# Twelve seven-product blocks instead of ten in the first feed-forward of an encoder layer, with a gate weight split earlier and the modulation work re-timed

## The chip, the cores and the metric

The kernel runs on one core of one Trainium2 chip. The metric is the device time in microseconds of one execution; lower is better.

## The reference

One layer of a streaming encoder on 544 tokens (512 of a prompt, 32 of a sample), width 1024. Shift, scale and gate vectors for three sublayers come from a conditioning vector per sequence:

```python
mod = silu(c) @ w_cond + b_cond                  # 9 pieces of 1024
sh1, sc1, gt1, sh2, sc2, gt2, sh3, sc3, gt3 = split(mod, 9)
x = LN(ALPHA*x + 0.5*(1+gt1) * swiglu(x*(1+sc1)+sh1, f1_gate, f1_up, f1_down))   # d_ff = 2816
x = LN(ALPHA*x +     (1+gt2) * mixer(x*(1+sc2)+sh2, w_in) @ w_out)
x = LN(ALPHA*x + 0.5*(1+gt3) * swiglu(x*(1+sc3)+sh3, f2_gate, f2_up, f2_down))

def swiglu(h, w_gate, w_up, w_down):
    return (silu(h @ w_gate) * (h @ w_up)) @ w_down
```

The mixer has four retention heads and eight heads of attention over keys that an indexer selects (at most 128 or 136 per query), all fed by one input projection `w_in` of 33 column blocks of 128. Everything is float32.

## The kernel before

**Layout and precision.** Activations lie transposed: 128 features on the partitions, 544 tokens along the free axis, in two halves of 272. A float32 operand is kept as two parts, `hi` and `lo`, and each product of a 128x128 weight block with 272 tokens is three matmuls (hi·hi, hi·lo, lo·hi). One pass of eight weight blocks over one half is so 24 matmuls.

**Weights.** `ensure`, `next_w` and `split_w` stream 128-column weight blocks: SyncE (SP) loads the raw block, ScalarE (ACT) casts it to `hi`, then either ScalarE writes the negated `hi` into `lo` and a DMA issued by GpSimd (POOL) adds the raw weight from memory onto it, or VectorE (DVE) subtracts. `next_w(n)` sees to it that n blocks beyond the one asked for have been given out for splitting; the default is `AHEAD = 3`. Split blocks lie in a pool `wh` of five buffers; most other large tiles (activations, residual, hidden blocks, modulation weights) are units of a pool `up` of 35.

**Seven products.** A feed-forward has 22 blocks f of 128 hidden features. An ordinary block (`ffn_mm` four times: gate and up, two halves each) is 96 matmuls. For the blocks in `SEVEN[0]` (first feed-forward, f = 6 to 15) and `SEVEN[1]` (second, f = 4 to 21), `feed` takes gate and up weight, split in two along the input features, with the two token halves as a 2x2 problem and does it by seven products of 12 matmuls (Strassen's scheme in Winograd's form), 84 in all. For this, activation sums (`sums`, once) and weight sums (`weight_sums`, four VectorE additions in place on the raw weights, then `split_sums`, two splits) are made. In `seven(f)` the products come in this order, each 12 matmuls: C (gate weight `Wg`), onto A (`Wg2`), B (`Wu2`), onto A (`Wu2`), A of the next block (`begin`, its `Wg`), onto A (`Wg2`), onto B (`Wu`, written `wh_u`). Short copies of A by ScalarE (`snapshot`, L713) and additions by VectorE (L763, L780, L794) take results out between them; a bank is written again only after these have read it. Inside `feed` the order of the ScalarE and VectorE instructions is pinned by hand. `make_gate(f)` is the cast (L683), the negation (L678) and the accumulating DMA (L679, tile `wh_g`) of a block's gate weight; in steady state it runs for block f + 2 at the start of block f. Ahead of the first seven-product block (`first7`), `make_gate(first7)` runs in block first7 - 2, and `make_gate(first7 + 1)`, `weight_sums(first7)` and `split_sums` in block first7 - 1. The results of these blocks stay unsplit in `flat` tiles, two to a unit; `split_flat` splits one per tick after the last seven-product block.

**Order.** The program is written out in one order; `tick()` is called after every pass of products, and jobs (generators given to `spawn`) resume at ticks and yield the number of ticks to their next step. A seven-product block has four ticks, as an ordinary block has. All SP loads, and all TensorE instructions, stay in program order; other instructions are placed by a scheduler with the program's order as priority.

**Modulation.** `cond` computes pieces 2 to 6 of `mod` on VectorE: per piece eight steps (one for each 128 rows of `w_cond`), each two multiply-adds of 128x1024 (L589; the first step of a piece L587), then `cond_done`: one tick apart four transposes with a sum each (L552, L553), and four ticks later a small matmul (`cc`). A list of gaps sets the ticks between steps. Piece 7 is made by `cond_ahead` during the input projection, piece 8 later. `consts` turns finished pieces into coefficients.

**After the feed-forward** come its down-projection (`proj_residual`, tile `dn`, residual tiles `xa` loaded by `scaled_residual`), the layer norm into `h2`, the input projection (`project`, tile `in`) interleaved with retention, indexer, selection and attention (`lg` are its logits), the output projection and the second feed-forward.

Of the kernel before, what the change touches and what calls it, by code (L numbers as in the profile page):

```python
# [18 lines left out]
ND = D // P  # L19
# [5 lines left out]
NF = FF // P  # L25
# [6 lines left out]
SEGS = ((((0, HT), 0),), (((HT, TP), 0), ((TP, T), 1)))  # L32
DOWN_G = ((0, 8), (8, 15), (15, 22))
AHEAD = 3
SEVEN = ((6, 15), (4, NF - 1))
WHOLE = (2, 8)


# [1 line left out]
def encoder_layer_kernel(ctx, tc, xT, cT, wc1, w_e, w_cond, b_condT, lnp, w_gu1, w_dn1, w_in, w_out, w_gu2, w_dn2,  # L40
# [32 lines left out]
    def load(*a):  # L73
        ordered("load", nc.sync.dma_start(*a))
# [12 lines left out]
    def resume(job, base):  # L87
        n = next(job, None)
        if n is not None:
            jobs.append((base + n, job))  # L90

    def spawn(job):
        resume(job, now[0] + 1)
# [14 lines left out]
    lp = const.tile([P, 6, ND], F32, name="lp")  # L108
# [8 lines left out]
    def mod(r, m):  # L117
        return modT[:, r, 8 * m:8 * m + 8]
# [42 lines left out]
    def ensure(n):  # L161
        while len(split) < n and stream and stream[0]:
            if not fetched:
                fetch_ahead()
            src, cnt, kw = stream.pop(0)
            split.append(split_w(fetched.pop(0), cnt, "w", src=src, **kw))

    def next_w(ahead=AHEAD):
        ensure(1 + ahead)
        return split.pop(0)  # L170
# [209 lines left out]
    def small(name):  # L380
        return const.tile([P, ND], F32, name=name)

    def mod_consts(n, msh, msc, lg, lb):
        G, B = [], []
        for r in range(2):
            g, bb = small(f"G{n}{r}"), small(f"B{n}{r}")
            nc.vector.tensor_scalar(g, mod(r, msc), 1.0, None, op0=ALU.add)
            nc.vector.tensor_mul(bb, g, lb)
            nc.vector.tensor_add(bb, bb, mod(r, msh))
            nc.vector.tensor_mul(g, g, lg)  # L390
            G.append(g)
            B.append(bb)
        return G, B

    def gate_coef(n, m, c):
        out = []
        for r in range(2):
            g = small(f"C{n}{r}")
            nc.vector.tensor_scalar(g, mod(r, m), c, c, op0=ALU.mult, op1=ALU.add)
            out.append(g)  # L400
        return out
# [12 lines left out]
    def queue_ffn(w_gu, w_dn, first):  # L414
        for f in range(2, NF):
            seven = SEVEN[0 if first else 1]
            if not seven[0] <= f <= seven[1]:
# [148 lines left out]
    def cond(parts, gaps):  # L566
        todo = [(m, d) for m in parts for d in range(ND)]
        ws, accs = [], {}

        def fetch():  # L570
            if len(ws) < len(todo):
                m, d = todo[len(ws)]
                ws.append(up.tile([P, 1024], F32, name=f"wc{m}_{d}", tag="u"))
                load(ws[-1], w_cond[d * P:(d + 1) * P, 1024 * m:1024 * m + 1024])

        fetch()
        yield 1
        fetch()
        yield 2
        for n, (m, d) in enumerate(todo):  # L580
            if d == 0:
                accs[m] = [up.tile([P, 1024], F32, name=f"ca{m}_{r}", tag="u") for r in range(2)]
            fetch()
            for r, acc in enumerate(accs[m]):
                c = cz[:, d, r:r + 1]
                if d == 0:
                    got = nc.vector.tensor_scalar(acc, ws[n], c, None, op0=ALU.mult)  # L587
                else:
                    got = nc.vector.scalar_tensor_tensor(acc, ws[n], c, acc, op0=ALU.mult, op1=ALU.add)  # L589
                tc.add_manual_dep(got.ins, last["pe"], NOSYNC, reason="pace")  # L590
            if d == ND - 1:
                spawn(cond_done(m, accs[m]))
            yield gaps[n % len(gaps)]

    def cond_ahead(m):
        acc = [up.tile([P, 1024], F32, name=f"ca{m}_{r}", tag="u") for r in range(2)]

        def part(d):
            return w_cond[d * P:(d + 1) * P, 1024 * m:1024 * m + 1024]

        def add(d, w):
            for r in range(2):
                c = cz[:, d, r:r + 1]
                if d == 0:
                    n = nc.vector.tensor_scalar(acc[r], w, c, None, op0=ALU.mult)
                else:
                    n = nc.vector.scalar_tensor_tensor(acc[r], w, c, acc[r], op0=ALU.mult, op1=ALU.add)
                tc.add_manual_dep(n.ins, last["pe"], NOSYNC, reason="pace")

        ws = [up.tile([P, 1024], F32, name=f"wc{m}_{d}", tag="u") for d in range(4)]  # L610
        for d in range(4):
            nc.gpsimd.dma_start(ws[d], part(d))
        yield 6
        for d in range(4):
            add(d, ws[d])
            yield 1
        yield 14
        for d in range(4, ND):
            ws.append(up.tile([P, 1024], F32, name=f"wc{m}_{d}", tag="u"))
            load(ws[d], part(d))  # L620
        for d in range(4, ND):
            add(d, ws[d])
            yield 5 if d < ND - 1 else 5
        spawn(cond_done(m, acc))

    def later(n, job):
        yield n
        yield from job

    def known(*ms):  # L630
        assert all(("mod", m) in flags for m in ms), ms
# [33 lines left out]
    def feed(h, hid, sums, flat, begun, gu, blocks, whole, lead=None):  # L665
# [4 lines left out]
        def load_gate(f):  # L670
            raw_g[f] = fetch_w(gu[f, 0], ND, "g")
# [9 lines left out]
        def make_gate(f):  # L681
            Wg[f] = wh.tile([P, 2, ND, P], FR, name="wh_g", tag="wh")
            pin(nc.scalar.copy(Wg[f][:, 0], raw_g[f]))  # L683
            negated(Wg[f][:, 0], Wg[f][:, 1], gu[f, 0])
# [31 lines left out]
        first7, last7 = blocks  # L716
# [92 lines left out]
        for f in range(2, first7):  # L809
            place(f)  # L810
            if f == first7 - 2:
                load_gate(first7)
                load_up(first7)
            if f == first7 - 1:
                load_gate(first7 + 1)
                load_up(first7 + 1)
                load_gate(first7 + 2)
            st = [None, None], {}
            for which in range(2):
                for i in range(2):  # L820
                    ffn_mm(st, h, which, i)
                    if f == first7 - 2 and which == 0:
                        if i == 0:
                            make_gate(first7)
                        else:
                            make_up(first7, 0)
                            make_up(first7, 1)
                    if f == first7 - 1:
                        if which == 0 and i == 1:
                            weight_sums(first7)  # L830
                        if which == 1 and i == 0:
                            split_sums(first7, Wg2, raw_g)
                            split_sums(first7, Wu2, raw_u)
                            make_gate(first7 + 1)
            for i in range(2):
                ffn_act(st, hid[f] if f < whole else None, i, flat.get(f))
        assert stream.pop(0) is None
# [12 lines left out]
        for i in range(2):  # L850
            ffn_act(sts[f], hid[f], i)
    flat, following = {}, ([None, None], {})
    spawn(later(4, cond((2, 3, 4, 5, 6), [3] * 4 + [4] * 10 + [2] * 12 + [2, 3] * 7)))
    feed(h, hid, sums, flat, None, w_gu1, SEVEN[0], WHOLE[0], lambda: ffn_mm(following, h, 0, 0))
    hid.extend([None] * len(flat))

# [7 lines left out]
    spawn(split_flat())  # L864
    for f in range(SEVEN[0][1] + 1, NF):
        hid.append(unit("hid", FR))
# [9 lines left out]
    G2, B2, C2, G3, B3 = [], [], [], [], []  # L876

    def consts(ready, *made):
        while not flags.issuperset(("mod", m) for m in ready):
            yield 1  # L880
        for dst, src in made:
            for got, new in zip(dst, src()):
                got.extend(new)

    spawn(consts((3, 4), ((G2, B2), lambda: mod_consts(2, 3, 4, lp[:, 0, :], lp[:, 1, :]))))
    spawn(consts((5, 6, 7), ((G3, B3), lambda: mod_consts(3, 6, 7, lp[:, 2, :], lp[:, 3, :])),
                 ((C2,), lambda: [gate_coef(2, 5, 1.0)])))

    h, rs, fin = ln_to_h(xr, G2, B2, "h2_", 4, 1)
    proj_residual(hid, xr, C1, DN, fin, ahead={(6, 15): 7, (7, 0): 6, (7, 8): 5, (7, 15): 4})  # L890
# [2 lines left out]

    xd = nc.dram_tensor("x_spill", [4, P, 2 * T], F32, kind="Internal").ap()

    def project(evac):
        hl = next_w()
        for i, (a, b) in enumerate(HALVES):
            ps = bank("a", "in")[:, :HT]
            for k in range(ND):  # L900
                mm3(ps, hl, k, h[k], a, b, k == 0, k == ND - 1)
            evac(ps, a, b)
            tick()
# [562 lines left out]
        tick()  # L1466


    known(5, 6, 7)
    h, rs, fin = ln_to_h(xr, G3, B3, "h3_", 3, 4)  # L1470
    proj_residual(mixed, xr, C2, OUT, fin, [("sample", 1)], ahead={(d, 0): min(5, 11 - d) for d in range(ND)})

# [38 lines left out]
    spawn(later(9, cond((8,), [4])))  # L1511
    feed(h, hid, sums, flat, begun, w_gu2, SEVEN[1], WHOLE[1])
    for f in range(WHOLE[1], NF):
# [155 lines left out]
```

## Time and profile before

| | us |
|---|---|
| median of 3 runs | 1152.5 |
| lowest and highest run | 1150.21, 1157.97 |
| the profiled execution, its own time | 1150.75 |
| span of that execution in the trace | 1149.0 |

The mean granted TensorE clock over the span was 0.993 of full speed. Times of instructions are counted from the start of the span; about 1.75 us of the execution lie around it. PE is TensorE's matmuls, PEld its weight loads, which run beside them. In the rows below, "xN" counts instructions that are merged into one row, and a bracket gives the idle time of the engine just before the row and what ended it. A PE row's length contains the pipeline's tail, so rows of PE overlap a little; the chain's rows do not.

### The profile page before, as it was taken

How to read it: one execution, taken by the hardware profiler on the slowest of the kernel's cores; microseconds unless marked ns; L12 is line 12 of the kernel's file. 1: busy time of each engine (PE TensorE's matmuls, PEld its weight loads, DVE VectorE, ACT ScalarE, POOL GpSimd, SP SyncE). 2: the span in 40 equal slices, each digit the busy share in tenths (PEclk: the TensorE clock that was granted, in tenths of full speed). 3: DMA queues.
4: the chain of work that ended last, by engine and by line, in shares of the span. 5: the costliest groups of instructions: out<-in, count | busy, mean ns of one | idle time of the engine just before them, and what ended most of it. 6: DMA issues, size and time to landing. Idle time of an engine off the chain costs nothing.

```text
span 1149.0 us, 22815 instructions
## 1 busy us (share of the span) xinstructions
PE 1116.0 (97%) x9083; PEld 1082.9 (94%) x9083; DVE 835.3 (73%) x1758; ACT 635.8 (55%) x1102; POOL 195.2 (17%) x219
## 2 busy tenths in 40 slices
PE   8998999999999999999989999999999999999995
PEld 7998999999999999989979989999999999999995
DVE  5576898686679686788999777789699976810416
ACT  3644666651434345765655758645666666753523
POOL 0110111111110301523211100100111111051110
PEclk9998999999999999999999999999999999999998
DMA  9897778985997547765954767871888687478742
GB/s 359 268 269 200 190 214 208 294 244 160 315 277 173 138 177 149 193 173 138 265 130 104 178 226 203 213 219 19 211 234 221 153 191 184 131 218 183 172 82 79
DMA packets 71452, 222.75 MB, mean 194 GB/s; under 512 B 8656, under 2 KB 12880, under 8 KB 71344
## 3 DMA queue, kind: packets, MB, share of 16 engines
q1 hardware_dynamic: 49456, 151.02, 37.6%
q0 software_dynamic: 21744, 70.13, 34.0%
q8 instruction: 71, 1.16, 0.4%
q14 instruction: 37, 0.30, 0.1%
q10 hardware_dynamic: 144, 0.14, 0.0%
HBM read 209.66 MB, written 9.58 MB: 191 GB/s over the span
## 4 chain that ended last, share of the span: by engine, by line
PE 74%; DMA 8%; DVE 8%; issue 6%; ACT 2%; SPq 0%; POOL 0%; DVEq 0%; POOLq 0%; ACTq 0%
PE dn L77 24%; PE in L77 12%; PE pA L77 11%; PE gu L77 11%; PE pB L77 5%; DMA we_raw<-in_w_e 3%; PE pC L77 3%; PE gu_e L77 2%; DMA wh_g<-in_w_gu 2%; DMA aqk<-rp 1%; DMA wc<-in_w_cond 1%; DMA wh_w<-in_w_dn 1%; DVE wh_s L702 1%; PE isc L77 1%; PE po L77 1%
## 5 line engine op out<-in xcount | busy, mean ns | idle before, releaser
L77 PE MATMUL dn<-hid,wh_w 128*128 128x272 f32 x2112 | 267.2, 288 | 0.7 <-DMA wh_w<-in_w_dn 0.5
L77 PEld LDWEIGHTS dn<-hid,wh_w 128*128 128x128 f32 x2112 | 265.4, 188 | 1.3 <-DMA wh_w<-in_w_dn 0.7
L77 PE MATMUL in<-h,wh_w 128*128 128x272 f32 x1392 | 187.0, 291 | 1.4 <-DMA wh_w<-in_w_in 1.4
L77 PEld LDWEIGHTS in<-h,wh_w 128*128 128x128 f32 x1392 | 176.6, 188 | 6.9 <-issue 3.5
L131 ACT CAST wh_w<-wr_w 128x1024 fp32r<-128x1024 f32 (+1 forms) x106 | 107.1, 1015 | 114.3 <-PE dn L77 75.9
L77 PE MATMUL gu<-h,wh_w 128*128 128x272 f32 x1152 | 145.2, 288 | 0.0
L77 PEld LDWEIGHTS gu<-h,wh_w 128*128 128x128 f32 x1152 | 144.6, 188 | 0.0
L589 DVE SCALAR_TENSOR_TENSOR ca<-wc,cz,ca 128x1024 f32<-128x1024 f32 x84 | 106.5, 1290 | 0.0
L77 PE MATMUL pA<-hs,wh_s 128*128 128x272 f32 x672 | 94.0, 289 | 1.5 <-ACT s L713 1.4
L77 PEld LDWEIGHTS pA<-hs,wh_s 128*128 128x128 f32 x672 | 87.4, 188 | 2.4 <-ACT s L713 2.4
L138 ACT ACTIVATE wh_w<-wh_w 128x1024 fp32r<-128x1024 f32 (+1 forms) x86 | 87.9, 1027 | 1.7
L286 DVE SCALAR_TENSOR_TENSOR xs<-dn,C,xs 128x272 f32<-128x272 f32 (+2 forms) x24 | 9.0, 404 | 81.6 <-PE dn L77 81.6
L679 POOL DMA_DIRECT2D wh_g<-in_w_gu x28 | 24.4, 871 | 232.0 <-ACT wh_g L678 129.4
L713 ACT COPY s<-pA 128x272 f32<-128x272 f32 x84 | 32.1, 382 | 55.5 <-PE pA L77 54.8
L139 POOL DMA_DIRECT2D wh_w<-in_w_dn x32 | 28.2, 880 | 165.8 <-ACT wh_w L138 120.1
L77 PE MATMUL pA<-h,wh_g 128*128 128x272 f32 x336 | 48.4, 293 | 5.3 <-DMA wh_g<-in_w_gu 5.3
L77 PEld LDWEIGHTS pA<-h,wh_g 128*128 128x128 f32 x336 | 45.0, 192 | 5.7 <-DMA wh_g<-in_w_gu 5.7
L139 POOL DMA_DIRECT2D wh_w<-in_w_in x29 | 25.3, 873 | 136.1 <-ACT wh_w L138 78.1
L77 PE MATMUL pA<-h,wh_s 128*128 128x272 f32 x336 | 47.4, 291 | 0.0
L702 DVE TENSOR_TENSOR wh_s<-wr_g,wh_s 128x1024 fp32r<-128x1024 f32 x28 | 34.3, 1224 | 17.3 <-ACT wh_s L701 17.3
L77 PE MATMUL pC<-h,wh_g 128*128 128x272 f32 x336 | 46.5, 287 | 0.0
L77 PE MATMUL pB<-hs,wh_u 128*128 128x272 f32 x336 | 46.4, 287 | 0.0
(329 smaller groups left out, 2022.2 us busy)
## 6 DMA issues: line engine op xcount, KB each, us to landing
wc<-in_w_cond SPq DMA_DIRECT2D x52, 512.0 KB, 6.1
wr_w<-in_w_in SPq DMA_DIRECT2D x33, 512.0 KB, 5.3
wh_w<-in_w_in POOLq DMA_DIRECT2D x29, 512.0 KB, 6.6
wr_w<-in_w_gu SPq DMA_DIRECT2D x28, 512.0 KB, 6.9
wr_g<-in_w_gu SPq DMA_DIRECT2D x28, 512.0 KB, 3.5
wr_u<-in_w_gu SPq DMA_DIRECT2D x28, 512.0 KB, 4.4
wh_g<-in_w_gu POOLq DMA_DIRECT2D x28, 512.0 KB, 6.5
wr_w<-in_w_dn SPq DMA_DIRECT2D x32, 448.0 KB, 3.9
```

What stands on the lines that cost most here:

```text
L77: ordered("pe", nc.tensor.matmul(*a, **kw))
L131: c = nc.scalar.copy(hi[:, :n, :], raw[:, :n, :])
L138: nc.scalar.mul(lo[:, :n, :], hi[:, :n, :].bitcast(F32), -1.0)
L139: nc.gpsimd.dma_start(lo[:, :n, :], src, accum_op=ALU.add)
L286: nc.vector.scalar_tensor_tensor(x[:, sa:sb], ps[:, sa - a:sb - a], coef[r][:, d:d + 1], x[:, sa:sb], op0=ALU.mult, op1=ALU.add)
L589: got = nc.vector.scalar_tensor_tensor(acc, ws[n], c, acc, op0=ALU.mult, op1=ALU.add)
L679: nc.gpsimd.dma_start(lo, src, accum_op=ALU.add)
L702: pin(nc.vector.tensor_tensor(W[f][:, 1], raw[f], W[f][:, 0].bitcast(F32), op=ALU.subtract))
L713: pin(nc.scalar.copy(s, ps))
```

## The change

- `SEVEN[0]` becomes (6, 17): twelve blocks of the first feed-forward by seven products instead of ten; four ordinary blocks follow instead of six.
- `make_gate(first7 + 1)` moves two passes earlier, ahead of `weight_sums(first7)` and `split_sums`. This is inside `feed` and so in both feed-forwards.
- The gaps of `cond` change: six ticks instead of four after piece 2's last step, four and three after steps 14 and 15, and two throughout after that.
- The last yield of `cond_ahead` is 20 instead of 5: piece 7's `cond_done` starts 15 ticks later.
- The coefficients that need piece 5 alone are made apart from those that need 6 and 7, and an assertion at build time that all three are known is dropped.
- The first three calls of `project` ask for four weights ahead instead of three.

```diff
-SEVEN = ((6, 15), (4, NF - 1))
+SEVEN = ((6, 17), (4, NF - 1))
...
         for d in range(4, ND):
             add(d, ws[d])
-            yield 5 if d < ND - 1 else 5
+            yield 5 if d < ND - 1 else 20
         spawn(cond_done(m, acc))
...
                     if f == first7 - 1:
+                        if which == 0 and i == 0:
+                            make_gate(first7 + 1)
                         if which == 0 and i == 1:
                             weight_sums(first7)
                         if which == 1 and i == 0:
                             split_sums(first7, Wg2, raw_g)
                             split_sums(first7, Wu2, raw_u)
-                            make_gate(first7 + 1)
...
-    spawn(later(4, cond((2, 3, 4, 5, 6), [3] * 4 + [4] * 10 + [2] * 12 + [2, 3] * 7)))
+    spawn(later(4, cond((2, 3, 4, 5, 6), [3] * 4 + [4] * 3 + [6] + [4] * 6 + [4, 3] + [2] * 24)))
...
-    spawn(consts((5, 6, 7), ((G3, B3), lambda: mod_consts(3, 6, 7, lp[:, 2, :], lp[:, 3, :])),
-                 ((C2,), lambda: [gate_coef(2, 5, 1.0)])))
+    spawn(consts((5,), ((C2,), lambda: [gate_coef(2, 5, 1.0)])))
+    spawn(consts((6, 7), ((G3, B3), lambda: mod_consts(3, 6, 7, lp[:, 2, :], lp[:, 3, :]))))
...
+    early_w = [4, 4, 4]
+
     def project(evac):
-        hl = next_w()
+        hl = next_w(early_w.pop() if early_w else AHEAD)
...
-    known(5, 6, 7)
     h, rs, fin = ln_to_h(xr, G3, B3, "h3_", 3, 4)
```

## The prediction

> **What bounds the kernel now.** First the page: busy shares, then the chain that ended last.
>
> ```profile
> span 1149.0 us, 22815 instructions
> PE 1116.0 (97%) x9083; PEld 1082.9 (94%) x9083; DVE 835.3 (73%) x1758; ACT 635.8 (55%) x1102; POOL 195.2 (17%) x219
> PE 74%; DMA 8%; DVE 8%; issue 6%; ACT 2%; SPq 0%; POOL 0%; DVEq 0%; POOLq 0%; ACTq 0%
> ```
>
> TensorE is busy for 97% of the span, so there are only two ways to gain: fewer matmuls, or less of the 33 us in which it stands. The second view is TensorE's list of waits (total, times, longest):
>
> ```profile
> PE pA L77 <- DMA wh_g<-in_w_gu: 5.3, 2, 4.5
> PE lg L77 <- DVE mx L1274: 4.3, 4, 1.4
> PE in L77 <- DMA wh_w<-in_w_in: 1.4, 1, 1.4
> PE pA L77 <- ACT s L713: 1.4, 3, 0.6
> PE dn L77 <- DMA wh_w<-in_w_dn: 0.5, 1, 0.5
> PE dn L77 <- DVE wh_w L141: 0.2, 1, 0.2
> ```
>
> One entry stands out: two waits for a gate weight, the longer 4.5 us. The timeline of TensorE there, a window (length; busy of PE, PEld, DVE, ACT, POOL; then the granted clock), and the chain's account:
>
> ```profile
> 103.00 0.41 PE L77 MATMUL pA<-h,wh_g 128*128 128x272 f32 x2
> 107.88 2.63 PE L77 MATMUL pA<-h,wh_g 128*128 128x272 f32 x10 [4.47 <-DMA wh_g<-in_w_gu]
> ...
> 107.88:112.93 5.05, 5.05 (x24) 5.05 (x25) 1.01 (x1) 1.33 (x2) 0.00 (x0) 0.55 1.05 292
> ...
> 98.59 9.25 DMA wh_g<-in_w_gu
> ...
> 107.88 5.05 PE pA L77 x22
> ...
> 848.81 4.52 PE pA L77 x36
> ```
>
> The gate weight of the second seven-product block left POOL at 98.59 and landed 9.25 us later. Two matmuls ran on its first part, then TensorE stood 4.47 us. Afterwards the granted clock was 0.55: 22 matmuls took 5.05 us, where 36 take 4.52 us (0.1256 each) in the second feed-forward. 22 x 0.1256 = 2.76, so the slow clock cost another 2.29 us. The wait is worth **6.76 us**, not 4.47.
>
> **The change part by part.** *Gate weight ahead.* Why was it late? ScalarE's queue, and the load of the raw weight:
>
> ```profile
> 71.48 0.33 SPq L74 DMA_DIRECT2D wr_g<-in_w_gu  x1
> ...
> 86.11 0.40 ACT L201 ACTIVATE tnh<-gu 128x272 f32<-128x272 f32 x1 [1.22 <-PE gu L77]
> 89.11 0.40 ACT L201 ACTIVATE tnh<-gu 128x272 f32<-128x272 f32 x1 [2.59 <-PE gu L77]
> 94.00 1.05 ACT L701 CAST wh_s<-wr_g 128x1024 fp32r<-128x1024 f32 x1 [4.49 <-DVE wr_g L697]
> 94.95 1.04 ACT L701 CAST wh_s<-wr_u 128x1024 fp32r<-128x1024 f32 x1
> 95.90 1.04 ACT L683 CAST wh_g<-wr_g 128x1024 fp32r<-128x1024 f32 x1
> ...
> 97.12 1.06 ACT L678 ACTIVATE wh_g<-wh_g 128x1024 fp32r<-128x1024 f32 x1
> ```
>
> Its raw form was asked for at 71.48, long before. Its cast (95.90) and negation (97.12) stood behind the two casts of weight sums, which waited 4.49 us for VectorE. In its new place, after the first product pass of block 5, which ended just before 86.11, they meet a ScalarE that idled 2.59 us ahead of 89.11: 86.5 + 1.04 + 1.06 = 88.6, and even with the slow landing of 9.25 us the weight is there at 98, 5 us before 103.00. POOL has nothing queued in that stretch. Of the five weight buffers block 5's two and block 6's gate are taken; the weight takes one of the other two, and the weight sums take the last and the one of block 5's gate, which is done before 89.11. Behind the two ScalarE operations waits the Silu of 89.11, 2.1 us at most if they come late, and its bank has a spare. Later weights move up with the products. All 6.76 goes. In the second feed-forward the same move meets:
>
> ```profile
> 818.79 1.52 PE L77 MATMUL pA<-h,wh_g 128*128 128x272 f32 x10 [0.80 <-DMA wh_g<-in_w_gu]
> ```
>
> The weight comes two passes (6 us) earlier; **0.80** goes.
>
> [...]
>
> *Two more blocks by seven products.* From the chain:
>
> ```profile
> 212.82 42.09 PE gu L77 x336
> ...
> 842.83 1.49 PE pB L77 x12
> ...
> 853.32 1.49 PE pB L77 x12
> ```
>
> A plain block is 4 x 24 = 96 matmuls, at 42.09 / 336 = 0.1253 each: 12.03 us. A seven-product block is 84, and from one block to the next passes 853.32 - 842.83 = 10.49 us. Two blocks: 2 x 1.54 = **3.08 us**. That holds where VectorE keeps up: one block's window, and one piece of modulation.
>
> ```profile
> 134.00:144.50 10.50, 10.50 (x86) 10.50 (x85) 9.25 (x13) 6.82 (x12) 1.74 (x2) 1.00 0.85 225
> ...
> 168.87 2.48 DVE L589 SCALAR_TENSOR_TENSOR ca<-wc,cz,ca 128x1024 f32<-128x1024 f32 x2
> ```
>
> VectorE needs 9.25 us of 10.50, a 2.48 us piece included. That is tight but fits, for twelve blocks as for ten, with one piece each.
>
> *Pieces shifted.* Two of the three waits on "ACT s" come while part 2's transposes and the pieces of part 3 meet on VectorE:
>
> ```profile
> 161.46 1.76 PE L77 MATMUL pA<-hs,wh_s 128*128 128x272 f32 x12 [0.55 <-ACT s L713]
> ...
> 173.00 1.26 PE L77 MATMUL pA<-hs,wh_s 128*128 128x272 f32 x8 [0.54 <-ACT s L713]
> ```
>
> The new gap of six ticks puts two more ticks (a tick is one step of the schedule, four to a block) between; both waits could go (gain 1.1). But from there each piece falls half a block later: behind the weight sums instead of ahead of the first addition. What queues behind it is the addition L780, which reads bank B before TensorE may write it again:
>
> ```profile
> 119.65 0.69 DVE L697 TENSOR_TENSOR wr_g<-wr_g 128x512 f32<-128x512 f32 x1
> 120.90 0.44 DVE L780 TENSOR_TENSOR up<-s,pB 128x272 f32<-128x272 f32 x1 [0.57 <-ACT s L713]
> ...
> 123.30 1.65 PE L77 MATMUL pB<-hs,wh_u 128*128 128x272 f32 x12
> ```
>
> 120.34 + 2.48 + 0.44 = 123.26, against 123.30: it just fits. Six full pieces at up to 0.3 us each would cost 1.8. Between +1.1 and -1.8 I take **+0.5**, since the transposes' waits are in the trace and the new one is not.
>
> *Ahead by four.* The first three projections ask for one weight more: a cast, a negation and a DMA each, earlier but not more. The one wait (1.4) is for the first projection's weight, whose place in the order stays. Taken at nothing; bounds 0 and 1.4 gained.
>
> *Part 7's transposes 15 ticks later* (four transposes with a sum each; the first two transposes are this row):
>
> ```profile
> 613.22 1.29 DVE L552 STREAM_TRANSPOSE ctr<-ca 128x512 f32<-128x512 f32 x2
> ```
>
> TensorE does not wait there, so leaving gains little; where they arrive, attention's last softmaxes also use VectorE. Some 5 us of VectorE change place and I charge nothing; bounds plus and minus 1.5, about a third of the 4.3 us on "lg". Making one constant apart, and the dropped assertion, cost nothing.
>
> *End of the first feed-forward.* After the change 16 blocks instead of 14 are split, in 16 ticks instead of 24. VectorE before, in the plain blocks:
>
> ```profile
> 206.00:257.00 51.00, 51.00 (x410) 51.00 (x409) 37.07 (x58) 31.32 (x48) 7.45 (x9) 1.00 0.95 265
> 257.00:282.00 25.00, 25.00 (x202) 25.00 (x201) 18.16 (x22) 3.80 (x8) 3.73 (x4) 1.00 0.49 130
> ```
>
> 55.2 us, less two pieces: 50.3 to fit in 16 x 3.0 = 48 us. VectorE runs full, some us late. TensorE has two or three banks per product and tolerates that. I charge nothing; bounds 0.7 gained (both waits on "dn") and 2 lost (the cap worked out under the last rival).
>
> **Sum:** 6.76 + 0.80 + 3.08 + 0.5 = 11.1. 1150.75 - 11.1 = 1139.6 from the profiled run, whose time lies 1.75 below the median of 1152.5 (1141.4 from there). I say 1140.5, between the two.
>
> **Rivals.** *More goes* (0.16): half of the 4.3 on "lg" and the 1.4 on the projection weight go too, since both stand where edits were made: 11.1 + 3.6 = 14.7, 1136. Against it: no instruction ahead of these waits is removed.
>
> *VectorE takes TensorE's place* (0.14): the piece in front of L780 is late by half its length, 1.24 us, in each of six blocks: 7.4 us back, 1147. For it: 0.04 us of margin. Against it: without a piece ahead of the block's first addition, everything behind starts earlier.
>
> *The gate weight is not early* (0.05): ScalarE's order puts its casts where they were. Only 3.6 is left: 1147. Against it: the casts are pinned in program order.
>
> *The slow clock is not in every run* (0.05): if the ordinary run pays the wait but not the half rate, the change gains 8.8 there: 1142. [...] Against it: no time shown is 2.29 below the profiled run.
>
> *Slower* (0.06): the down-projection's weights come late.
>
> ```profile
> 264.85 15.55 SPq L74 DMA_DIRECT2D xa<-in_xT  x8
> 280.49 0.38 SPq L74 DMA_DIRECT2D wr_w<-in_w_dn  x1
> ...
> 275.50 1.30 DVE L552 STREAM_TRANSPOSE ctr<-ca 128x512 f32<-128x512 f32 x2
> ```
>
> SP's queue is in order. Eight loads of the residual stretch over 15.55 us for want of free units, and the weights behind them leave at 280.49, just in time (waits 0.5 and 0.2). Part 4's transposes, which free two units, ran from 275.50. By the lists of gaps part 4's last piece comes 75 ticks after the first one instead of 70, so they are five ticks (5 x 3.0 = 15 us) later now. If the last residual load waits for them, TensorE stands 15 us and then runs slowly (2.3): 17.3 - 11.1 = 6 slower, 1157. It decides from 11 us of delay on. Against it: the eight units of h come free with the last up-product, at 212.82 + 23 x 24 x 0.1253 = 282.0 by the chain's row above, 1.5 us after 280.49, which caps the delay at some 2 us; and with two blocks still unsplit fewer units are taken.
>
> **How the numbers follow.** The forecast, 1137.5 to 1143, has 0.54. About 1% (11.5 us) is what a measurement can tell from no change, and it lies inside: 0.28 of the 0.54 goes beyond it, with the 0.16 of "more": faster 0.44. Slower by over 1% needs the last rival at its worst, 0.03. Range: down to 1135 for most of "more", up to 1147.5 for the 7.4 us returned.
>
> **What would show it.** In the trace after: no wait of TensorE on wh_g and clock 1.0 throughout the feed-forwards; 84 matmuls in 10.5 us in twelve blocks; waits of pB on VectorE near zero from the ninth block on; the weights of the down-projection leaving SP before the last up-product ends. I am wrong if a wait above 3 us stands at the start of the down-projection, or if a block from the ninth on lasts over 11 us.

## The result and the profile after

The changed kernel took 1138.47 us (median of 4, 1136.67 to 1141.46) beside 1151.86 us for the kernel before on the same chip (median of 4): a ratio of 0.9878 with a 95% interval of 0.9856 to 0.9900. Run again unchanged with the second set of experiments it gave 0.9892 (0.9874 to 0.9911). The forecast was 1140.5 us, range 1135.0 to 1147.5.

The profiled execution of the changed kernel is the slowest of its four, 1141.46 us; two of its waits are looked at below. First the page of the changed kernel: span, busy shares, the chain, and two groups of matmuls (busy time, mean ns of one | idle time before them).

```profile
span 1139.6 us, 22804 instructions
PE 1112.5 (98%) x9059; PEld 1081.3 (95%) x9059; DVE 848.4 (74%) x1772; ACT 637.9 (56%) x1110; POOL 197.9 (17%) x219
...
PE 86%; DMA 6%; DVE 5%; ACT 2%; issue 1%; SPq 0%; DVEq 0%; ACTq 0%
...
L77 PE MATMUL dn<-hid,wh_w 128*128 128x272 f32 x2112 | 266.6, 288 | 0.0
...
L77 PE MATMUL pA<-hs,wh_s 128*128 128x272 f32 x720 | 100.3, 288 | 0.0
```

There are 24 matmuls fewer (9059 against 9083), as two blocks of 84 instead of 96 need. TensorE's part of the chain rose from 74 to 86%: work of other engines fell out of the path. The products `pA` with the sums and those of the down-projections wait for nothing any more; before, the rows ended in 1.5 and 0.7.

Next, the rows around the gate weight of the second seven-product block in the changed kernel: ScalarE, then the start of its DMA on POOL, then TensorE (start, length).

```profile
86.48 0.40 ACT L201 ACTIVATE tnh<-gu 128x272 f32<-128x272 f32 x1 [1.22 <-PE gu L77]
86.78 1.04 ACT L683 CAST wh_g<-wr_g 128x1024 fp32r<-128x1024 f32 x1
87.85 1.06 ACT L678 ACTIVATE wh_g<-wh_g 128x1024 fp32r<-128x1024 f32 x1
89.47 0.40 ACT L201 ACTIVATE tnh<-gu 128x272 f32<-128x272 f32 x1 [0.56 <-PE gu L77]
94.37 1.05 ACT L701 CAST wh_s<-wr_g 128x1024 fp32r<-128x1024 f32 x1 [4.49 <-DVE wr_g L697]
...
89.31 0.87 POOL L679 DMA_DIRECT2D wh_g<-in_w_gu  x1 [4.66 <-ACT wh_g L678]
...
101.30 1.67 PE L77 MATMUL pA<-hs,wh_s 128*128 128x272 f32 x12
102.81 1.67 PE L77 MATMUL pA<-h,wh_g 128*128 128x272 f32 x12
104.32 1.66 PE L77 MATMUL pA<-h,wh_s 128*128 128x272 f32 x12
```

The cast and the negation took the idle 2.59 us ahead of the next `tnh` (0.56 of it are left), the DMA left POOL 9.28 us earlier than before, and the twelve matmuls that used to be broken after two (wait 4.47 us) run through at 1.51 us from pass to pass. The cast of the weight sums still waits the same 4.49 us for VectorE, now with nothing behind it that is late.

The stages, cut at the first matmul of each: from the first seven-product block to the down-projection, the down-projection, and the mixer (from the first `project` to the output projection); the stretch before the first `project` is the same in both, 24.95 us, and is left out. Columns: window, its length; busy time of PE, PEld, DVE, ACT, POOL; granted clock; DMA share; GB/s. Before:

```profile
94.92:282.02 187.10, 181.15 (x1423) 180.00 (x1421) 149.01 (x207) 105.11 (x167) 29.47 (x33) 0.98 0.81 218
282.02:417.30 135.28, 134.59 (x1070) 133.99 (x1069) 99.31 (x165) 53.15 (x73) 23.51 (x23) 1.00 0.74 213
...
442.26:708.77 266.51, 258.34 (x2135) 235.83 (x2134) 215.47 (x666) 165.30 (x337) 57.48 (x69) 1.00 0.68 176
```

After:

```profile
95.29:270.37 175.08, 175.05 (x1398) 174.79 (x1397) 149.13 (x207) 104.97 (x172) 33.95 (x33) 1.00 0.86 228
270.37:404.40 134.03, 134.03 (x1070) 133.87 (x1069) 110.87 (x182) 53.10 (x75) 22.91 (x22) 1.00 0.74 214
...
429.35:700.91 271.56, 261.12 (x2132) 238.46 (x2131) 216.04 (x654) 165.35 (x337) 55.48 (x69) 0.99 0.66 173
```

In the first feed-forward TensorE is now busy in 175.05 of 175.08 us at clock 1.00: nothing is left to gain there but matmuls. It is 12.0 us shorter. The same cuts in the runs that the argument needs (us; "FFN1" is the first of these stages, "FFN2" the seven-product part of the second feed-forward):

| kernel | FFN1 | down-projection | mixer | FFN2 |
|---|---|---|---|---|
| before | 187.10 | 135.29 | 266.51 | 187.23 |
| after | 175.09 | 134.03 | 271.56 | 186.14 |
| after, run again | 175.04 | 134.03 | 271.12 | 186.14 |
| gate weight alone | 180.01 | 134.53 | 268.49 | 186.14 |
| twelve blocks alone | 183.35 | 134.08 | 268.60 | 187.08 |
| four ahead alone | 186.54 | 134.09 | 271.31 | 186.87 |
| after, old gaps | 177.00 | 134.08 | 267.63 | 186.14 |

A stage in which TensorE no longer waits repeats to 0.1 us (175.0, 186.14). With waits left in it the same code of a stage takes different times in different traces: the feed-forwards by some 0.5 us, the down-projection by 1.2 to 1.8, the mixer by 5 (266.85 to 272.09 us among the kernels below that share the mixer of the kernel after). By stages the profiled runs of before and after differ by 12.0 + 1.1 + 1.3 - 5.0 + 0.1 (the rest) = 9.4 us (spans 1149.0 and 1139.6), while the medians differ by 13.4. The 12.0 and 1.1 belong to the change; the other two are looked at below.

### The profile page after: what moved, and what is told of

It is laid out like the page before. It is cut to its first block, busy times and chain, and to the rows that moved or that the text cites. A ratio compares the mean times of both kernels' runs of the same rounds, so it can differ in the third digit from the quotient of the medians.

```text
span 1139.6 us, 22804 instructions
## 1 busy us (share of the span) xinstructions
PE 1112.5 (98%) x9059; PEld 1081.3 (95%) x9059; DVE 848.4 (74%) x1772; ACT 637.9 (56%) x1110; POOL 197.9 (17%) x219
## 4 chain that ended last, share of the span: by engine, by line
PE 86%; DMA 6%; DVE 5%; ACT 2%; issue 1%; SPq 0%; DVEq 0%; ACTq 0%
PE dn L77 27%; PE pA L77 16%; PE in L77 12%; PE gu L77 11%; PE pB L77 8%; PE pC L77 4%; DMA we_raw<-in_w_e 3%; PE gu_e L77 2%; PE po L77 1%; PE pt L80 1%; PE lg L77 1%; DMA rp<-iqf 1%; PE ro L77 1%; DMA wr_w<-in_w_in 1%; PE isc L77 1%
## 5 line engine op out<-in xcount | busy, mean ns | idle before, releaser
L77 PE MATMUL in<-h,wh_w 128*128 128x272 f32 x1392 | 189.9, 293 | 3.4 <-DVE rqk L937 2.5
L131 ACT CAST wh_w<-wr_w 128x1024 fp32r<-128x1024 f32 (+1 forms) x102 | 102.9, 1014 | 100.6 <-PE dn L77 81.9
L77 PE MATMUL gu<-h,wh_w 128*128 128x272 f32 x960 | 121.1, 288 | 0.0
L77 PEld LDWEIGHTS gu<-h,wh_w 128*128 128x128 f32 x960 | 120.6, 188 | 0.0
L589 DVE SCALAR_TENSOR_TENSOR ca<-wc,cz,ca 128x1024 f32<-128x1024 f32 x84 | 107.6, 1300 | 0.0
L77 PE MATMUL pA<-hs,wh_s 128*128 128x272 f32 x720 | 100.3, 288 | 0.0
L77 PEld LDWEIGHTS pA<-hs,wh_s 128*128 128x128 f32 x720 | 93.7, 188 | 0.0
L138 ACT ACTIVATE wh_w<-wh_w 128x1024 fp32r<-128x1024 f32 (+1 forms) x82 | 83.7, 1026 | 1.5
L77 PE MATMUL pB<-hs,wh_u 128*128 128x272 f32 x360 | 49.8, 287 | 0.0
L77 PE MATMUL pC<-h,wh_g 128*128 128x272 f32 x360 | 49.8, 287 | 0.0
L77 PE MATMUL pB<-hs,wh_s 128*128 128x272 f32 x360 | 49.8, 287 | 0.0
```

Source lines behind the costliest of these rows:

```text
L77: ordered("pe", nc.tensor.matmul(*a, **kw))
L131: c = nc.scalar.copy(hi[:, :n, :], raw[:, :n, :])
L138: nc.scalar.mul(lo[:, :n, :], hi[:, :n, :].bitcast(F32), -1.0)
```

## The experiments

**Which part earned it?** Each part of the change but one was put alone into the kernel before, or taken alone out of the kernel after; the coefficients made apart were not tested by themselves, and the new gaps only as a whole.

*The gate weight alone* (kernel before with one line moved):

```diff
+                        if which == 0 and i == 0:
+                            make_gate(first7 + 1)
                         if which == 0 and i == 1:
                             weight_sums(first7)
...
-                            make_gate(first7 + 1)
```

> The kernel before with only the gate weight of the second seven-product block made two passes earlier, in both feed-forwards. By the sum of the prediction: no wait on wh_g, the granted clock 1.0 there, and 6.76 + 0.80 = 7.6 us less, 1144.3. Rival (the half clock is not in every run): 5.3 us less. Rival (the stall gave VectorE time that it then lacks): waits on ACT s grow, and only 5 to 6 us are gained.

Measured: 1145.54 against 1152.27 us, ratio 0.9931 (0.9907 to 0.9954), half of the whole gain. Its first feed-forward is 7.09 us shorter and its second 1.09. No wait on the gate weight is left in it; the waits on "ACT s" are two instead of three:

```profile
PE pA L77 <- ACT s L713: 1.2, 2, 0.6
```

*Twelve blocks alone:*

```diff
-SEVEN = ((6, 15), (4, NF - 1))
+SEVEN = ((6, 17), (4, NF - 1))
```

> The kernel before with only twelve blocks by seven products instead of ten; gate weight, gaps of the modulation and the rest as before. By the block count alone: 3.1 us less, with the 4.5 us wait on wh_g still there. Rival (VectorE has no room without the new gaps): three or more waits on ACT s, 2 to 4 us given back, so a time about that of before.

Measured: 1148.53 us, ratio 0.9968 (0.9952 to 0.9985); the stage is 3.75 us shorter. Its waits:

```profile
PE pA L77 <- DMA wh_g<-in_w_gu: 5.0, 2, 4.3
...
PE pA L77 <- ACT s L713: 1.4, 3, 0.6
```

Both old waits are there, so the two blocks pay without the new gaps. Of the 3.75 some 0.6 is a shorter stretch of slow clock after the wait, which the next run shows too without any change to the feed-forward; beside that run the blocks give 186.54 - 183.35 = 3.19. Where neither kernel has a slow clock there, they give 3.01: 180.01 with the gate weight alone against 177.00 in the kernel after with the old gaps (below).

*Four ahead alone:*

```diff
+    early_w = [4, 4, 4]
...
-        hl = next_w()
+        hl = next_w(early_w.pop() if early_w else AHEAD)
```

> The kernel before with only the first three projections asking for four weights ahead. Theory A: slower than before by 2 to 5 us (1154 to 1157), with a wait of TensorE on the rope product that the kernel before does not have. Rival B: within 1.5 us of before.

Measured: 1152.31 us, ratio 0.9994 (0.9978 to 1.0011): no effect that these times can show. And taken out of the kernel after (`early_w = []`):

> The changed kernel with the first three projections asking for three weights ahead again. Theory A (the extra weight load and its accumulating DMA slow the small rope transfers, VectorE waits for them and TensorE then waits 2.5 us on VectorE at the second half of the second projection): the rope gathers land about 10 us after the projections start instead of 13, the 2.5 us wait on the rope product goes, and the time falls by 2 to 5 us, to about 1134 to 1136. Rival B (the new waits in the projection are a chance of the profiled run, which was the slowest of four): the time stays within 1.5 us of 1138.5 and a wait of 2 us may stand there or not. In both the first feed-forward stays at 175 us.

Measured: 1140.90 us, ratio 0.9894 (0.9873 to 0.9916), within the intervals of the changed kernel. This run was made because of new waits in the mixer of the profiled run of after (448.82 and 471.50 below), for which the three earlier weights were a suspect. The three weights are not what makes these waits: the unchanged kernel, run again, has neither, and the kernels with the gate weight alone and with the twelve blocks alone have the one of 2.2 us without any earlier weight.

> The changed kernel once more, as it is. If the new waits of its first trace (2.5 us on the rope product, 2.2 us on the copy of rv, two half-clock stretches in the mixer) belong to the change, they stand here again and the mixer takes 271 us or more from the first single projection to the output projection. If they are chance, they differ, and the time is 1138 give or take 1.5. The first feed-forward takes 175.1 us either way.

Measured: 1140.19 us, ratio 0.9892; the waits of TensorE in its trace:

```profile
PE lg L77 <- DVE mx L1277: 3.9, 3, 1.4
PE in L77 <- DMA wh_w<-in_w_in: 1.8, 1, 1.8
PE lg L77 <- ACT aqs L947: 1.3, 1, 1.3
```

The two waits are not there, which the expectation took for a sign of chance; but the mixer took 271.12 us, which it took for a sign of the change. What makes up the length differs: four stretches of 3.41 us at half clock here, two in the first trace. Whether the change has a share in it these two traces don't tell.

*The old gaps in the kernel after:*

```diff
-[3] * 4 + [4] * 3 + [6] + [4] * 6 + [4, 3] + [2] * 24
+[3] * 4 + [4] * 10 + [2] * 12 + [2, 3] * 7
```

> The changed kernel with the old gaps of the modulation. If the shift of the pieces is worth the 0.5 us of the prediction, the first feed-forward takes 175.6 us. If it removed all the waits on ACT s, about 1.8 us: 176.9, with these waits back. If twelve blocks have no room without it (the rival), several us: 178 to 181.

Measured: 1139.82 us, ratio 0.9898 (0.9880 to 0.9916): the times can't tell it from the kernel after, but the stage can: 177.00 against 175.05, as expected if the shift had removed all the waits (176.9), and the two waits on "ACT s" are back. TensorE in this run:

```profile
152.24 1.66 PE L77 MATMUL pB<-hs,wh_s 128*128 128x272 f32 x12
154.51 1.77 PE L77 MATMUL pA<-hs,wh_s 128*128 128x272 f32 x12 [0.62 <-ACT s L713]
156.12 1.66 PE L77 MATMUL pA<-h,wh_g 128*128 128x272 f32 x12
...
163.86 1.66 PE L77 MATMUL pB<-hs,wh_s 128*128 128x272 f32 x12
166.05 1.77 PE L77 MATMUL pA<-hs,wh_s 128*128 128x272 f32 x12 [0.54 <-ACT s L713]
167.66 0.54 PE L77 MATMUL pA<-h,wh_g 128*128 128x272 f32 x3
```

Read the starts, not the brackets: two passes take 156.12 - 152.24 = 3.88 and 167.66 - 163.86 = 3.80 us where undisturbed ones take 3.00 (101.30 to 104.32 above: 3.02). Each wait costs 0.8 to 0.9, not the 0.62 and 0.54 in its bracket, which begins only at the modelled end of the pass before. Some 0.3 more goes in smaller delays that have no bracket.

*Part 7's late finish taken out* (the last yield 5 again):

> The changed kernel with part 7's transposes at their old place, 15 ticks earlier. By the prediction nothing within 1.5 us. If those transposes held up attention's softmaxes, the waits on lg grow by 1 to 2 us and the time with them. If their new place is the worse one, 1 to 2 us less.

Measured: 1137.98 us, ratio 0.9889 (0.9865 to 0.9913): no difference that these times can show.

**How far does it go?** If two blocks give 3.1 us, do two more?

```diff
-SEVEN = ((6, 17), (4, NF - 1))
+SEVEN = ((6, 19), (4, NF - 1))
...
-[3] * 4 + [4] * 3 + [6] + [4] * 6 + [4, 3] + [2] * 24
+[3] * 4 + [4] * 3 + [6] + [4] * 6 + [4, 4] + [2] * 24
...
-            yield 1
+            if f % 2:
+                yield 1
```

> Fourteen blocks of the first feed-forward by seven products (f = 6 to 19), piece 3's last step one tick later, and two blocks split per tick after them; otherwise the changed kernel. By the block count another 3.08 us: 172.0 us for the first feed-forward and 1135. Rival: VectorE and the units run short at the start of the down-projection, where 18 blocks are then split in 9 ticks, and TensorE waits there for hid or for weights: the gain is given back, 1138 or more.

Measured: 1144.12 us, ratio 0.9940 (0.9918 to 0.9961). The first feed-forward gave the 3.05 us (172.02), and the down-projection took 144.50 instead of 134.03. Its waits, then two windows: the start of the down-projection, and the slow clock in it; last, the first of the two windows again for the modulation's multiply-adds (L589) alone:

```profile
PE dn L77 <- DVE hid L663: 3.3, 2, 1.9
...
PE dn L77 <- ACT hid L661: 0.9, 1, 0.9
PE dn L77 <- DVE wh_w L141: 0.9, 1, 0.9
...
266.78:292.00 25.22, 19.80 (x125) 18.47 (x124) 24.45 (x32) 15.78 (x25) 1.77 (x2) 0.82 0.64 202
...
282.80:293.04 10.24, 7.93 (x33) 7.61 (x34) 9.94 (x13) 5.13 (x6) 1.77 (x2) 0.50 0.89 249
...
266.78:292.00 25.22, 9.96 (x8) 0.82 0.64 202
```

VectorE is busy in 24.45 of 25.22 us, 9.96 of them with the modulation, while it owes TensorE the split blocks; and behind waits of which none is over 2 us the clock stood at half for 10.24 us. Is it the modulation pieces that stand in the way, or the few ticks left? Three kernels held part 4 back by 16 ticks instead of 4 or 3: with fourteen and with thirteen blocks (`(6, 18)`), both with two splits to a tick, and the kernel after itself as the control:

```diff
-[3] * 4 + [4] * 3 + [6] + [4] * 6 + [4, 4] + [2] * 24
+[3] * 4 + [4] * 3 + [6] + [4] * 6 + [4, 16] + [2] * 24
```

> The fourteen-block kernel with the third modulation part to run (part 4) held 16 ticks instead of 4 after the second, so that no modulation piece meets the splitting of the 18 flat blocks on VectorE. Theory VectorE-full: the 10.5 us lost at the start of the down-projection were VectorE doing pieces (about a dozen at 1.25 us a half) while TensorE needed split blocks; without them the down-projection takes 134 to 136 us again and the gain of the two more blocks (3.05) stays: 1136 to 1138, below the changed kernel's 1139. Rival tick-bound: the splits come too late because only two plain blocks (8 ticks) are left to spread them over, whatever else VectorE does: the down-projection stays at 141 or more, 1142 to 1145. The parts 4 to 6 end some 36 us later than before, at about 410, which is ahead of their use; if that is not so, a new wait shows at the in-projection.

> Thirteen blocks by seven products (17 flat blocks, three plain ones after them), splits two to a tick, part 4 held as in the fourteen-block kernel. Theory VectorE-full: 1.5 us less than the changed kernel in the first feed-forward and 134 in the down-projection: about 1137.5 to 1139. Rival tick-bound: with three plain blocks (12 ticks) about half of the 10.5 us is lost: 1142.

> The changed kernel with part 4 held 16 ticks instead of 3, as the control: with twelve blocks no wait stands at the start of the down-projection, so taking pieces away from there should give nothing: first feed-forward 175.0, down-projection 134.0, 1138 to 1141. Rival: the later parts 4 to 6 then lie beside the in-projection, where VectorE makes evictions, and cost 1 to 3 us: 1141 to 1143.

Measured: 1145.77, 1147.84 and 1150.28 us against 1154.52; ratios 0.9935 (0.9911 to 0.9958), 0.9954 (0.9937 to 0.9971) and 0.9966 (0.9949 to 0.9984). Each came out above what its theory gave, and above its rival by 0.8, 5.8 and 7.3 us, on a chip on which the kernel before is 2 us slower. Yet the stages answered: with fourteen blocks the first feed-forward takes 172.01 us and the down-projection 135.73, with thirteen 173.53 and 135.72, in the control 175.06 and 135.71. So the pieces were what held up the splits, not the ticks. The same time was lost one stage later. The fourteen-block kernel from the first projection to the single ones, and its waits:

```profile
402.31:437.42 35.11, 28.87 (x201) 28.04 (x200) 34.51 (x81) 17.05 (x37) 2.62 (x3) 0.90 0.56 192
...
PE pm L77 <- DVE S L264: 3.9, 2, 2.6
PE in L77 <- DVE h L367: 3.6, 1, 3.6
```

35.1 us instead of 24.95, in each of the three (35.10, 35.04, 35.00): VectorE is busy in 34.51 of 35.11 us, and the held pieces, the last of which begins at 408.94 us, met the statistics and the writing of `h2` there. The waits are 6.2 us of the loss (3.6 on `h` and 2.6 on `S`; the other 1.2 of that row lies in the down-projection), the rest is the clock at 0.90. The twelve-block control, which had nothing to win in the down-projection, shows that cost by itself.

The last run held part 4 by 14 ticks and then let the pieces follow every one and two ticks in turn, to end in time:

```diff
-[3] * 4 + [4] * 3 + [6] + [4] * 6 + [4, 4] + [2] * 24
+[3] * 4 + [4] * 3 + [6] + [4] * 6 + [4, 14] + [1, 2] * 12
```

> Fourteen blocks with part 4 held 14 ticks, as in the held kernel, and the 24 pieces of parts 4 to 6 then every one and two ticks in turn instead of every two, so that they end at about 370 as in the changed kernel, ahead of the normalization at 390 to 405. In the kernel held 16 ticks the down-projection was whole again (135.7), and the same time came back behind it: pieces to 409, waits of 3.9 on S and 3.6 on h, 35.1 us from the first projection to the single ones instead of 24.95. Theory: the place of the pieces alone makes both: now first feed-forward 172.0, down-projection 134 to 136, 24.95 behind it, 1135 to 1138, below the changed kernel. Rival: a piece every 4.5 us is too dense for the DMA engines (share 0.9 there) or for VectorE (30 of 40 us): weights or evictions come late in the down-projection, 137 or more, and the time is 1139 to 1143.

Measured: 1137.84 us (1136.29 to 1139.46) against 1152.30, ratio 0.9872 (0.9843 to 0.9901). Its pieces end at 370 us, the stretch to the single projections is 24.95 again, and the down-projection:

```profile
266.74:402.78 136.04, 134.39 (x1071) 134.03 (x1069) 121.09 (x191) 51.71 (x73) 22.05 (x22) 1.00 0.77 223
...
PE cc L77 <- DVE red L553: 1.7, 1, 1.7
```

Of the 3.05 us that the two blocks give, 2.0 goes in the down-projection, most of it in one wait of the small matmul that ends a modulation piece. This kernel is as fast as the changed one; that it is faster the intervals don't show.

## Why the prediction was right

**Gate weight, forecast 6.76 + 0.80; measured 7.09 + 1.09.** This is shown by the run with it alone. The wait and the slow clock behind it both went, and one of the three short waits on "ACT s" with them. By the starts of the passes the 24 matmuls from 103.00 to 112.77 (shown in the last section) took 9.77 us before, and with the gate weight alone 3.00: 6.77 for the wait and the clock. The prediction came to the same sum by luck, since two slips cancel: the bracket of 4.47 leaves out 0.16 us of the wait, and the 5.05 counts the tail of the last matmul, 0.16, to the clock. The other 0.3 fits the short wait, whose bracket before is 0.29. Against the second trace of the same stage, 186.54 with four ahead alone, the gain is 6.5, because that run paid less for the clock (1.63 us against 2.13, in the last section). In the second feed-forward the bracket was 0.80 and the stage gained 1.09: the same undercount by brackets as in the old-gaps run. The rival "not early" (1147) fell with it.

**Two blocks, forecast 3.08; measured 3.0 to 3.2** and 3.05 for two more after them. VectorE's margin of 0.04 us ahead of L780 didn't decide. In the trace of after the two halves of a shifted piece stand among the weight sums, not behind them (186.31 and 188.11 in one block); L780 ends there at 190.35 and `pB` starts at 190.57. TensorE's matmuls of `pB` wait for nothing in after, and its weight loads for L780 once:

```profile
PEld pB L77 <- DVE up L780: 0.2, 1, 0.2
```

So the rival "VectorE takes TensorE's place" (1147) fell for twelve blocks. What it described, VectorE without room, came at fourteen, not at L780 but at the splits.

**Pieces shifted, forecast +0.5; measured +1.95.** This is the term that was mis-sized. I took the upper bound from the brackets (1.1), then went down for fear of the six pieces in front of L780, at 0.3 us each that I had from no row. The starts of the passes show that the two waits alone cost 1.7 us, and the one weight load above is all that came of the fear. My sum for the first feed-forward was 6.76 + 3.08 + 0.5 = 10.3; with 1.95 and the 7.09 it is 12.1, and 12.0 was measured.

**Ahead by four and part 7, forecast 0 and 0.** No run shows an effect of either, within some 2 us. **The end of the first feed-forward, forecast 0:** no wait stands at the start of the down-projection in after, and the slower rival (1157) didn't occur. SyncE after:

```profile
247.82 10.67 SPq L74 DMA_DIRECT2D xa<-in_xT  x8
258.53 0.43 SPq L74 DMA_DIRECT2D wr_w<-in_w_dn  x1
```

The residual loads stretch over 10.67 us instead of 15.55, and the first weight leaves 11.8 us before the down-projection begins at 270.37; before it left 1.5 us ahead of 282.02. The condition of that rival was not met: part 4's transposes run from 281.90 in after, 23 us behind the last residual load, which so did not wait for them. Neither of the two signs that I named for being wrong is there.

**The sum, forecast 11.1; measured 13.1** in the two feed-forwards, which is nearly the 13.4 between the medians. Of the 2.0 that were missing 1.45 is the mis-sized term and 0.6 the gate weight with the short wait. The median lies between my 1140.5 and the 1136 of the rival "more goes", but not by that rival's reason: the waits on "lg" and on the projection's weight, of which it let half and the whole go, are there in both runs of after (2.9 and 3.9 on `mx`; 0.9 and 1.8). The rival "slow clock not in every run" (1142) was wrong for the three traces that have the wait, each with half clock behind it, but it had a true core, shown in the last section: the price differs by half a microsecond.

The rest of what the two profiles show is not shown to be the change's. The down-projection of before takes 135.29 us in its profile, but 134.09 with four ahead alone, which has the same ten blocks; and the kernel without part 7's late finish showed 135.85 with twelve. In the mixer of the profiled run of after there are these two waits, and a half-clock stretch behind the second:

```profile
448.82 6.28 PE L77 MATMUL in<-h,wh_w 128*128 128x272 f32 x48 [2.50 <-DVE rqk L937]
...
471.50 0.28 PE L80 MATMUL rkt<-cm,rqk 128*32 128x128 f32 x1 [2.21 <-DVE rv L1142]
...
471.85:475.26 3.41, 3.41 (x16) 2.97 (x17) 2.82 (x9) 1.20 (x3) 1.34 (x1) 0.50 1.04 217
```

The mixer of after took 271.12 us in its second trace with other waits, 266.85 in the fourteen-block kernel and 272.09 in the twelve-block control, all three the same code. Why VectorE is late there in some runs and not in others stays open: the four weights ahead are not needed for it, and no run tested another cause. So it stays open, too, whether the change has a share in the mixer's 5 us. The medians leave little room for one: they give 13.4 (interval 11.5 to 16.6), of which the feed-forwards are 13.1.

## What to carry to other kernels

A wait inside a stream of matmuls costs the distance between the starts of the passes around it less the undisturbed distance (0.8 to 0.9 us in the run with the old gaps, with 0.62 and 0.54 in the brackets), so size it by those starts, with the slow clock behind it (1.63 and 2.13 us in the two runs of the last section), and not by the bracket. Work that is moved out of one engine's crowded stretch has to be followed to where it lands: holding the pieces cured the down-projection and cost 10 us at the layer norm behind it, and only held and packed denser did they fit. To find what a change of several parts earned, compare the stages of the traces; stages without waits repeated to 0.1 us where the runs of one kernel lie 2 to 8 us apart.

## What the runs showed of the hardware

The half clock behind the same wait cost differently from run to run. Before, the next pass behind the 22 slow matmuls, then three windows of 3.41 us around the wait, which lasted from 103.41 to 107.88 (the second column is PE's busy time, the third number from the end the granted clock):

```profile
112.77 1.67 PE L77 MATMUL pB<-hs,wh_u 128*128 128x272 f32 x12
...
102.18:105.59 3.41, 1.23 (x10) 1.01 (x9) 2.58 (x5) 1.43 (x2) 0.86 (x1) 1.00 1.01 262
105.59:109.01 3.42, 1.13 (x5) 1.13 (x6) 0.70 (x1) 0.00 (x0) 0.00 (x0) 0.50 1.07 211
109.01:112.42 3.41, 3.41 (x17) 3.41 (x17) 0.51 (x1) 1.33 (x2) 0.00 (x0) 0.50 1.05 302
```

In the kernel with four ahead alone, TensorE behind the same wait (103.15 to 107.55), and three such windows:

```profile
107.55 2.16 PE L77 MATMUL pA<-h,wh_g 128*128 128x272 f32 x10 [4.40 <-DMA wh_g<-in_w_gu]
109.50 2.61 PE L77 MATMUL pA<-h,wh_s 128*128 128x272 f32 x12
111.94 1.67 PE L77 MATMUL pB<-hs,wh_u 128*128 128x272 f32 x12
...
101.34:104.76 3.42, 1.81 (x14) 1.59 (x13) 2.60 (x5) 1.68 (x3) 0.86 (x1) 1.00 0.99 273
104.76:108.17 3.41, 0.62 (x5) 0.62 (x6) 1.23 (x1) 0.01 (x1) 0.00 (x0) 1.00 1.08 223
108.17:111.58 3.41, 3.41 (x18) 3.41 (x17) 0.47 (x1) 1.33 (x2) 0.00 (x0) 0.50 1.04 264
```

Before, the granted clock fell at 105.59 us and rose again at 112.42; the second and the third window are the two halves of that. In after it fell at 7.64, 471.85 and 584.49 us and rose again 3.41 us later each time. Around the wait of before TensorE was busy for 1.23 us in the first window, and the clock stayed down for 6.83 us from its end. With four ahead alone it was busy for 1.81 us in the first window; in the second the clock was still full, with 0.62 us of work, and only in the third it was at half, for 3.41 us. So the 22 matmuls took 4.39 us there (107.55 to 111.94) instead of 4.89 (107.88 to 112.77), and the clock cost 4.39 - 2.76 = 1.63 us instead of 2.13.

The slow stretches shown here lasted 3.41, 6.83 and 10.24 us. The length of a wait did not tell whether one follows: in after the wait of 2.50 us ahead of 448.82 was followed by full clock up to 471.84, the wait of 2.21 us ahead of 471.50 by half clock from 471.85 to 475.26. Nor did TensorE's busy time just before: in after 1.77 us in 444.54 to 447.95 was followed by full clock, 1.92 us in 581.07 to 584.49 by half. With fourteen blocks there were waits of 0.9 and 1.4 us with one matmul between them, and 10.24 us of half clock began in the second of these, at 282.80. What decides it, no run here shows.
